# Cached log-forget sums, decay factors and past convolution moved to the front of a decoder layer, with its adaLN loads and key pages rearranged

## The chip, the cores and the metric

One Trainium2 chip, one of its cores. The metric is device time in microseconds of one execution of the program on that core; several executions of each kernel are timed and their median is given. The engines are TensorE (PE; its weight loads are listed as PEld), VectorE (DVE), ScalarE (ACT), GpSimd (POOL) and SyncE (SP). Each runs its own instructions in the order in which the program lists them, and waits where an operand is not ready. SP, POOL and ACT also issue DMAs.

## The reference

One layer of a decoder trunk, for 512 prompt tokens and 8 sample tokens that share the weights (520 columns in all, width 1024, 16 heads of 64):

```python
sh1, sc1, g1, sh2, sc2, g2 = ada_modulation(c, ada_w, ada_b)      # silu(c) @ ada_w + ada_b
h = rms_norm(x, norm1_g) * (1.0 + sc1) + sh1
xr, gr, q, k, v, fl, ga, gb = jnp.split(h @ w_in, cuts, axis=-1)
xc, conv_new = causal_dwconv(xr, conv_buf, conv_w, conv_b)
hr, h_last = rg_lru(xc, h0, pos0, ...)          # log_a = -8 * gate_r * softplus(-lam)
ya = (hr * gelu(gr)) @ w_proj_a
yb = attend(q, k, v, log_sigmoid(fl + b_f)) @ w_proj_b
x = x + g1 * ((sigmoid(ga) * ya + sigmoid(gb) * yb) @ w_o)
x = x + g2 * SwiGLU(rms_norm(x, norm2_g) * (1.0 + sc2) + sh2)
```

The attention adds to each logit the sum of log f from the key to the query. A sample token attends to 1024 cached positions, 8 pages of 128 out of a pool of 80, picked by a page table; its keys, values and log f are read through that table.

## The kernel before

Activations lie with features on the partitions, as 8 tiles of 128 x 520. Every fp32 product is made of three fp32r products: ACT rounds an operand to a high part (whi, hh), DVE subtracts to get the low part (wlo, hl), and PE multiplies hi x hi, lo x hi and hi x lo in two column halves of 260. The weights are cut into units of 128 output columns; a unit's product takes PE 48 matmuls.

The start. SP loads the parameters (prm), constants (cs), x and the page table (ptb, idx); ACT squares x (sq), DVE adds the squares, PE sums them over the partitions (ss), ACT and DVE make the reciprocal root (r) and DVE normalises x (xn). Meanwhile eight pieces of ada_w (araw) come in through the pool pgp of seven buffers and PE makes the first half of the modulation from them (adaf, transposed in adaft). From these come mod and n1amp, then h (hh, hl). q is computed in two halves of the inner dimension: the first (qp) starts when four tiles of h and the first w_in pieces (wraw, split by `q_weights`) are there.

After q the units follow in a list written out by hand: xr (with its convolution on DVE, `conv`), ga, gb, gr, for eight tiles, with the RG-LRU's gates, exponentials and scans between them; then k, v and the attention; then pb, wo and the FFN (fig, fiu, fo). In the background runs the past of the sample tokens. At each of the first 42 units a step `tick` works off key pages that have landed (DVE multiplies a page by q, L663 and L667, and sums over each head, L664 and L668), lets softmax and value steps run, and issues as many key pages as the table KEYS says, on POOL's queue up to unit 40 and on SP's after it. The pages share the pool pgp with the ada_w pieces. `VALUES` lists the units at which a value page is used.

The pieces that the change moves:

- `past_load` (L369) fetches the log f of the 64 pages (lfp, 0.5 MB) with one indirect DMA on POOL, into one of the two wraw buffers. `past_turn` (L380) transposes it on PE (lft), copies it (lk), and POOL adds up, page by page from the last, what lies after each page (after). `past_sums` (L395) multiplies lk by a triangle and after by ones on PE (suf): the sum of log f from each key to the end. The softmax over the past first needs suf. They are called in the loop of q's units (i = 4, 6, 7) and after the first two gb units.
- `decay` (L599) makes from lambda the factors of the RG-LRU's exponent, with a polynomial `log1p` of small DVE operations on 128 x 8; first needed by `lru_exp`. `past_conv` (L807) makes the part of the convolution that the stored state gives; first needed in `conv`. Both are called at i = 6 of q's loop.
- `ada_load(1, 6)` issues the seventh ada_w piece of the second third of the modulation, after both gb units of the first round; `ada_piece(1, 6)` uses it on PE at the beginning of the next round.

The order in which instructions stand on each engine comes from a scheduler; it follows the code, but lets work that it holds ready go ahead.

Of the kernel before, what the change touches and what calls it, by code (L numbers as in the profile page):

```python
# [8 lines left out]
F32 = mybir.dt.float32  # L9
F32R = mybir.dt.float32r  # L10
I32 = mybir.dt.int32
# [8 lines left out]
NS = 8  # L20
# [4 lines left out]
KT = 8  # L25
# [39 lines left out]
def kernel(ctx, tc, xT, par, gates, b_f, cst, cse, own, cache_k, cache_v, cache_lf, pt,  # L65
# [103 lines left out]
    def flush():  # L169
        while stores:  # L170
# [1 line left out]

    later = {}

    KEYS = dict(zip(range(42), (2, 2, 2, 0, 3, 3, 3, 2, 1, 1, 1, 1, 2, 2, 2, 1, 0, 1, 0, 1, 2, 2, 2, 2, 1, 1, 1, 1, 2, 2, 1, 2,
                                1, 2, 1, 2, 1, 2, 1, 2, 1, 0)))
    VALUES = (19, 21, 23, 25, 27, 29, 31, 35, 37, 39)
    LAST_POOL = 40

# [180 lines left out]
        dve.tensor_scalar(t[:, t0:e_], t[:, t0:e_], amp[:, f, 0:1], mod[:, shf, f, 0:1], ALU.mult, ALU.add)  # L360


    ptb = keep.tile([1, NS * NPAGE], I32, name="ptb")
    sp.dma_start(ptb, pt.rearrange("a b -> (a b)")[None, :])
    idx = keep.tile([NS * NPAGE, 1], I32, name="idx")
    sp.dma_start(idx, pt.rearrange("a (b c) -> (a b) c", c=1))
    lfp = []

    def past_load():  # L369
# [100 lines left out]
    def wraw():  # L470
        return wp.tile([128, KT, 256], F32, name="wraw", tag="wraw", bufs=2)

    ssq = [bank(f"ss1_{j}") for j in range(2)]
    for f in range(KT):
        t = slot("sq1")
# [6 lines left out]
            for j, (t0, t1) in enumerate(HALVES):  # L482
                pe.matmul(ssq[j][:, :HALF], lhsT=ones, rhs=sq[:, t0:t1], start=f == 3, stop=f == KT - 1)
    acc = [bank(f"adaf{fh}") for fh in range(2)]
    first_mod(0, acc[0], range(KT))
    r1 = slot("r1")
    for j, (t0, t1) in enumerate(HALVES):
        act.activation(r1[:, t0:t1], ssq[j][:, :HALF], AF.Sqrt, bias=eps, scale=1.0 / D)
        dve.reciprocal(r1[:, t0:t1], r1[:, t0:t1])
    for f in range(KT):  # L490
        t = slot("xn")
        dve.tensor_tensor(t, x[f], r1, ALU.mult)
        xn.append(t)
# [28 lines left out]
    raw = wraw()  # L522
    q_weights(1, raw, 0, 4)
    load_chunks(0)
    sp.dma_start(cs[:, C_TRI:], cst[:, C_TRI:])


    def log1p(name, e, n, out):
        z, z2, t = (small(name + s, 128, n, 1) for s in "abc")
        dve.tensor_scalar(t, e, 2.0, None, ALU.add)  # L530
        dve.reciprocal(t, t)
        dve.tensor_tensor(z, e, t, ALU.mult)
        dve.tensor_tensor(z2, z, z, ALU.mult)
        dve.tensor_scalar(t, z2, 2.0 / 17.0, 2.0 / 15.0, ALU.mult, ALU.add)
        for k in (13, 11, 9, 7, 5, 3, 1):
            dve.tensor_tensor(t, t, z2, ALU.mult)
            dve.tensor_scalar(t, t, 2.0 / k, None, ALU.add)
        dve.tensor_tensor(out, t, z, ALU.mult)

    qtd = drp.tile([NS, D], F32, name="qtd")  # L540
    fld = drp.tile([H, NT], F32, name="fld")
# [47 lines left out]
    def sum_forget():  # L589
# [6 lines left out]
    cl = keep.tile([128, KT], F32, name="cl")  # L596
    cneg = keep.tile([128, KT], F32, name="cneg")

    def decay():  # L599
        le = small("le", 128, KT, 1)  # L600
        ll = small("ll", 128, KT, 1)
        act.activation(le, prm[:, :, P_LAM], AF.Abs)
        act.activation(le, le, AF.Exp, scale=-1.0)
        log1p("lz", le, KT, ll)
        dve.tensor_scalar(le, prm[:, :, P_LAM], -1.0, 0.0, ALU.mult, ALU.max)
        dve.tensor_tensor(le, le, ll, ALU.add)
        dve.tensor_scalar(cl, le, -8.0, None, ALU.mult)
        dve.tensor_scalar(cneg, le, 8.0, None, ALU.mult)


    S = []
# [193 lines left out]
    conv_past = keep.tile([128, KT, NS], F32, name="conv_past")  # L805

    def past_conv():  # L807
        t = slot("cvp", KT * 24).rearrange("p (k s n) -> p k s n", k=KT, s=NS)
        for i in range(KT):
            dve.tensor_tensor(t[:, i], prm[:, i, P_SC:P_SC + 24].rearrange("p (s n) -> p s n", n=3),  # L810
                              prm[:, i, P_CW:P_CW + 3].unsqueeze(1).to_broadcast([128, NS, 3]), ALU.mult)
        dve.tensor_reduce(conv_past, t, AX.X, ALU.add)

    gws = {}

    gate_raw = {}
# [163 lines left out]
    for i in range(0, KT, 2):  # L980
        conv(i)
        if i == 0:
            q_done(*q_last)
        else:
            if i == 2:
                ada_piece(1, 6)
                ada_load(1, 7)
            both(lru_root, i - 2)
            gelu(i - 2)
            lru_scan(i - 2)  # L990
        conv(i + 1)
        if i:
            if i == 2:
                ada_piece(1, 7)
                ada_copy(1)
            gelu(i - 1)
            lru_scan(i - 1)
            both(lru_mul, i - 2)
            both(lru_g, i - 2)
        if i < 6:  # L1000
            gate_a(i)
            lru_gates(i)
            if i == 2:
                ada_end(1)
            gate_a(i + 1)
            lru_gates(i + 1)
            gate_b(i)
            if i == 0:
                past_sums(0)
            gate_b(i + 1)  # L1010
            if i == 0:
                past_sums(1)
                ada_load(1, 6)
            both(lru_exp, i)
            if i == 2:
                log_forget()
            if i == 4:
                sum_forget()
        else:
            lru_gates(i)  # L1020
            gate_a(i)
            lru_gates(i + 1)
            gate_a(i + 1)
            both(lru_exp, i)
            gelu(i)
            both(lru_root, i)
            gelu(i + 1)
            both(lru_scan, i)
            both(lru_mul, i)
            both(lru_g, i)  # L1030
# [556 lines left out]
```

## Time and profile before

| | |
|---|---|
| runs | 1068.85, 1069.54, 1070.95 us; median 1069.54 |
| the profiled execution's own time | 1067.71 us, span 1066.1 us |
| busy in the span | PE 1021.3, DVE 664.0, ACT 494.2, POOL 202.2 us |
| mean granted clock of PE | 0.987 |
| DMA | 206.95 MB, 194 GB/s over the span |

Times are microseconds from the start of the span. A row of a wait list names the waiting engine and line, then what it waited for, then the total, the number of waits and the longest. A row of a timeline has start, duration, engine, line, operation, output<-input and count; in brackets stands the idle time before it and what ended it. A row of a tile's list has the number of instructions, then the shortest, median and longest duration in ns and the first and last start in us.

### The profile page before, as it was taken

The numbers are of one execution on the slowest core, as the hardware profiler recorded it, in microseconds if no ns is written. First come the engines' busy times: TensorE is split into PE (matmuls) and PEld (weight loads), VectorE is DVE, ScalarE is ACT, GpSimd is POOL, SyncE is SP. The second block draws the span as 40 slices with busy tenths as digits, with TensorE's granted clock in tenths as the row PEclk, the third lists the DMA queues.
The fourth block names the chain that finished last, engine by engine and source line by source line (L and its number), as shares of the span: only waits on it lengthen the run. The fifth ranks groups of instructions, "written<-read, shape, count | busy, mean of one in ns | idle before, by whom it ended". The sixth has DMA issues, their size and how long they took to land.

```text
span 1066.1 us, 21006 instructions
## 1 busy us (share of the span) xinstructions
PE 1021.3 (96%) x8210; PEld 948.1 (89%) x8210; DVE 664.0 (62%) x1166; ACT 494.2 (46%) x976; POOL 202.2 (19%) x348
## 2 busy tenths in 40 slices
PE   4999899999999999999999999999999999999994
PEld 2888779999998987888898989999999999999993
DVE  5447999988999986656765447733343333443363
ACT  4423565757782367767783235523212232123251
POOL 0224511112134234544400014100000000000022
PEclk9999899999999999999999999999999999999998
DMA  9898887778788998987746852232333332332212
GB/s 327 281 320 286 279 297 208 260 240 297 255 283 280 351 314 263 259 252 250 248 172 216 313 166 70 73 88 79 109 90 80 97 102 80 95 104 80 72 55 74
DMA packets 165285, 206.95 MB, mean 194 GB/s; under 512 B 9778, under 2 KB 126018, under 8 KB 165122
## 3 DMA queue, kind: packets, MB, share of 16 engines
q1 hardware_dynamic: 147746, 149.90, 45.6%
q0 software_dynamic: 13760, 49.29, 13.6%
q10 hardware_dynamic: 3680, 6.42, 1.6%
q8 instruction: 64, 1.05, 0.4%
q14 instruction: 35, 0.29, 0.1%
HBM read 192.49 MB, written 13.09 MB: 193 GB/s over the span
## 4 chain that ended last, share of the span: by engine, by line
PE 76%; DVE 9%; issue 4%; DMA 4%; ACT 4%; POOL 2%; POOLq 1%; SPq 0%; ACTq 0%; DVEq 0%
PE fiu L245 11%; PE fig L245 11%; PE fo L245 9%; PE pb L245 4%; PE k L245 4%; PE v L245 4%; PE pa L245 3%; PE gr L245 3%; PE gb L245 3%; PE ga L245 3%; PE xr L245 3%; PE wo L245 3%; PE pv L751 3%; DMA wraw<-in_w_in_dram 2%; PE qp L467 2%
## 5 line engine op out<-in xcount | busy, mean ns | idle before, releaser
L211 DVE TENSOR_TENSOR wlo<-wraw,whi 128x1024 fp32r<-128x1024 f32 (+1 forms) x131 | 160.7, 1227 | 159.3 <-ACT whi L210 153.2
L210 ACT CAST whi<-wraw 128x1024 fp32r<-128x1024 f32 (+1 forms) x131 | 136.7, 1043 | 242.7 <-PE fo L245 74.6
L337 POOL TENSOR_TENSOR ss<-ss,sq 128x260 f32<-128x260 f32 x18 | 13.6, 756 | 419.5 <-ACT sq L336 419.0
L245 PE MATMUL fiu<-h2h,wlo 128*128 128x260 f32 x320 | 90.5, 283 | 0.0
L245 PE MATMUL fig<-h2h,wlo 128*128 128x260 f32 x320 | 90.5, 283 | 0.0
L245 PE MATMUL fig<-h2l,whi 128*128 128x260 f32 x320 | 90.2, 282 | 0.0
L245 PE MATMUL fiu<-h2l,whi 128*128 128x260 f32 x320 | 90.2, 282 | 0.0
L245 PE MATMUL fig<-h2h,whi 128*128 128x260 f32 x320 | 90.2, 282 | 0.0
L245 PE MATMUL fiu<-h2h,whi 128*128 128x260 f32 x320 | 90.2, 282 | 0.0
L245 PE MATMUL fo<-ach,whi 128*128 128x260 f32 x292 | 82.8, 284 | 0.0
L245 PE MATMUL fo<-ach,wlo 128*128 128x260 f32 x292 | 82.5, 282 | 0.0
L245 PE MATMUL fo<-acl,whi 128*128 128x260 f32 x292 | 82.3, 282 | 0.0
L622 POOL DMA_DIRECT2D pg<-in_cache_k_dram x79 | 42.1, 533 | 115.8 <-DVE S L668 61.1
L245 PEld LDWEIGHTS fiu<-h2h,whi 128*128 128x128 f32 x320 | 60.2, 188 | 0.0
L245 PEld LDWEIGHTS fig<-h2h,whi 128*128 128x128 f32 x320 | 60.2, 188 | 0.0
L245 PEld LDWEIGHTS fig<-h2l,whi 128*128 128x128 f32 x320 | 60.2, 188 | 0.0
L245 PEld LDWEIGHTS fiu<-h2l,whi 128*128 128x128 f32 x320 | 60.2, 188 | 0.0
L245 PEld LDWEIGHTS fig<-h2h,wlo 128*128 128x128 f32 x320 | 60.1, 188 | 0.0
L245 PEld LDWEIGHTS fiu<-h2h,wlo 128*128 128x128 f32 x320 | 60.1, 188 | 0.0
L667 DVE TENSOR_TENSOR pg<-pg,qb 128x1024 f32<-128x1024 f32 x48 | 57.4, 1213 | 1.1 <-DMA pg<-in_cache_k_dram 1.0
L668 DVE TENSOR_REDUCE S<-pg 128x16 f32<-128x1024 f32 x48 | 57.2, 1207 | 0.0
L245 PEld LDWEIGHTS fo<-ach,wlo 128*128 128x128 f32 x292 | 55.1, 189 | 0.0
(388 smaller groups left out, 3445.6 us busy)
## 6 DMA issues: line engine op xcount, KB each, us to landing
araw<-in_ada_w_dram SPq DMA_DIRECT2D x48, 512.0 KB, 6.3
pg<-in_cache_k_dram POOLq DMA_DIRECT2D x47, 512.0 KB, 5.6
wraw<-in_w_fi_dram SPq DMA_DIRECT2D x44, 512.0 KB, 4.0
pg<-in_cache_v_dram SPq DMA_DIRECT2D x42, 512.0 KB, 4.9
wraw<-in_w_in_dram SPq DMA_DIRECT2D x34, 512.0 KB, 8.4
wraw<-in_w_in_dram SPq DMA_DIRECT2D x11, 1024.0 KB, 7.9
pg<-in_cache_v_dram POOLq DMA_DIRECT2D x22, 512.0 KB, 5.5
pg<-in_cache_k_dram POOLq DMA_DIRECT2D x32, 256.0 KB, 5.4
```

The costliest lines, as they stand in the source:

```text
L210: state["act"] = act.copy(hi[:, :k1 - k0], src)
L211: state["last"] = dve.tensor_tensor(lo[:, :k1 - k0], src, hi[:, :k1 - k0].bitcast(F32), ALU.subtract)
L245: state["mm"] = pe.matmul(out[:, :HALF], lhsT=wt[k], rhs=at, start=k == 0 and m == 0, stop=k == nk - 1 and m == 2)
L337: eng.tensor_tensor(acc[:, t0:t1], acc[:, t0:t1], q_, ALU.add)
L467: state["mm"] = pe.matmul(b[:, :HALF], lhsT=wt, rhs=at[:, t0:t1], start=k == 0 and m == 0, stop=k == 3 and m == 2)
L622: done.append(eng.dma_start(pg, cache[bass.ds(r, 1), :, c0:c1].rearrange("a p c -> (a p) c")))
L667: dve.tensor_tensor(pg, pg, q, ALU.mult)
L668: dve.tensor_reduce(S[r // 2][:, c:c + H], pg.rearrange("p (h d) -> p h d", d=DH), AX.X, ALU.add)
L751: pe.matmul(pv[0][32 * gq:32 * gq + 32, :], lhsT=pw[r][:, c:c + 32], rhs=pgs[gq // 2][:, 512 * hf:512 * hf + 512], start=j == 0, stop=j == ...
```

## The change

- The page table is loaded ahead of x instead of behind it, and 128 columns more of the constants (the triangle) come with the first load.
- `decay`, `past_conv` and `past_load` are called ahead of the sums of squares. `past_turn` for both halves stands ahead of the first modulation's matmuls, `past_sums(0)` after six and `past_sums(1)` after eight of the eight ada_w pieces.
- `ada_load(1, 6)` stands between the two gb units instead of behind them.
- KEYS: a key page moves from unit 29 to unit 16, and one from unit 33 to unit 40.

```diff
     sp.dma_start(prm, par)
-    sp.dma_start(cs[:, :C_TRI], cst[:, :C_TRI])
+    sp.dma_start(cs[:, :C_S16], cst[:, :C_S16])
+    ptb = keep.tile([1, NS * NPAGE], I32, name="ptb")
+    sp.dma_start(ptb, pt.rearrange("a b -> (a b)")[None, :])
+    idx = keep.tile([NS * NPAGE, 1], I32, name="idx")
+    sp.dma_start(idx, pt.rearrange("a (b c) -> (a b) c", c=1))
...
-    KEYS = dict(zip(range(42), (2, 2, 2, 0, 3, 3, 3, 2, 1, 1, 1, 1, 2, 2, 2, 1, 0, 1, 0, 1, 2, 2, 2, 2, 1, 1, 1, 1, 2, 2, 1, 2,
-                                1, 2, 1, 2, 1, 2, 1, 2, 1, 0)))
+    KEYS = dict(zip(range(42), (2, 2, 2, 0, 3, 3, 3, 2, 1, 1, 1, 1, 2, 2, 2, 1, 1, 1, 0, 1, 2, 2, 2, 2, 1, 1, 1, 1, 2, 1, 1, 2,
+                                1, 1, 1, 2, 1, 2, 1, 2, 2, 0)))
...
+    decay()
+    past_conv()
+    past_load()
     ssq = [bank(f"ss1_{j}") for j in range(2)]
...
     acc = [bank(f"adaf{fh}") for fh in range(2)]
-    first_mod(0, acc[0], range(KT))
     r1 = slot("r1")
...
+    past_turn(0)
+    past_turn(1)
+    first_mod(0, acc[0], range(6))
+    past_sums(0)
+    first_mod(0, acc[0], range(6, KT))
+    past_sums(1)
     for f in range(KT):
         t = slot("xn")
...
         if i == 4:
-            past_load()
             split_upto(1)
             close = forget_logits()
         if i == 6:
             close()
-            with tc.issue_after(state["last"].ins), tc.issue_after(state["act"].ins):
-                decay()
-                past_conv()
-            past_turn(0)
-        if i == 7:
-            past_turn(1)
...
             gate_b(i)
             if i == 0:
-                past_sums(0)
+                ada_load(1, 6)
             gate_b(i + 1)
-            if i == 0:
-                past_sums(1)
-                ada_load(1, 6)
```

(The definitions of `log1p`, `decay` and `past_conv` move up in the file, unchanged.)

How it moves instructions. DVE at the start, from the reciprocal of the norm (r) to the first low part of h (hl), before:

```order
L489 RECIPROCAL r_192<-r_192 128x260 x2
L492 TENSOR_TENSOR xn<-x,r_192 128x520 x8
L429 TENSOR_TENSOR mod<-adaft_223,prm 128x2x2x9 x2
L433 SCALAR_TENSOR_TENSOR n1amp<-mod,prm 128x36
L458 TENSOR_TENSOR wlo<-wraw,whi 128x512 x2
```

and after the change:

```order
L528 RECIPROCAL r_192<-r_192 128x260 x2
L458 TENSOR_TENSOR wlo<-wraw,whi 128x512 x2
L458 TENSOR_TENSOR wlo<-wraw,whi 128x1024
L537 TENSOR_TENSOR xn<-x,r_192 128x520 x8
L458 TENSOR_TENSOR wlo<-wraw,whi 128x1024
L429 TENSOR_TENSOR mod<-adaft_321,prm 128x2x2x9 x2
L433 SCALAR_TENSOR_TENSOR n1amp<-mod,prm 128x36
```

The low parts of the first two weight pieces (three wlo) now stand ahead of the eight normalisations xn, and a third piece's ahead of mod.

PE at the start, from the sums of squares (ss) to q's first matmul (qp), before:

```order
L483 MATMUL ss_0_114<-sq_129,cs 128x260
L483 MATMUL ss_1_115<-sq_129,cs 128x260
L416 MATMUL adaf_142<-araw,silc 32x256 x32
L425 MATMUL adaft_223<-cs,adas 128x128 x2
L467 MATMUL qp_0_276<-hh,whi 128x260
```

and after the change:

```order
L523 MATMUL ss_1_163<-sq_177,cs 128x260
L383 MATMUL lft_197<-cs,lfp 128x64 x7
L383 MATMUL lft_217<-cs,lfp 128x64 x8
L416 MATMUL adaf_190<-araw,silc 32x256 x16
L398 MATMUL suf_273<-lk,cs 128x512
L416 MATMUL adaf_190<-araw,silc 32x256 x4
L398 MATMUL suf_290<-lk,cs 128x512
L416 MATMUL adaf_190<-araw,silc 32x256 x12
L399 MATMUL suf_273<-after,cs 128x512
L399 MATMUL suf_290<-after,cs 128x512
L425 MATMUL adaft_321<-cs,adas 128x128 x2
L467 MATMUL qp_0_374<-hh,whi 128x260
```

The transposes of the cached log f (lft) stand ahead of the first adaf, and the sums over what comes after each page (suf<-after) ahead of adaft and q.

SP's queue around the seventh and eighth ada_w pieces, which are loads (1, 6) and (1, 7), before:

```order
L186 DMA wraw<-in_w_in_dram 128x8x128 x4
L186 DMA wraw<-in_w_in_dram 128x8x256
L296 DMA araw<-in_ada_w_dram 128x1024 x4
L186 DMA wraw<-in_w_in_dram 128x8x256
L171 DMA mtd<-st 32x1
```

and after the change:

```order
L190 DMA wraw<-in_w_in_dram 128x8x128 x2
L622 DMA lf<-lfd 16x520
L300 DMA araw<-in_ada_w_dram 128x1024 x2
L190 DMA wraw<-in_w_in_dram 128x8x256
L300 DMA araw<-in_ada_w_dram 128x1024 x2
L190 DMA wraw<-in_w_in_dram 128x8x256
L175 DMA mtd<-st 32x1
```

The first two of the four araw loads went ahead of a load of weights.

More of the change, by code (lines that the diff above doesn't have):

```diff
@@ L360, in modulate @@
         dve.tensor_scalar(t[:, t0:e_], t[:, t0:e_], amp[:, f, 0:1], mod[:, shf, f, 0:1], ALU.mult, ALU.add)
[L363 to L366, printed above, removed]
     lfp = []
@@ L471, in wraw, with log1p, decay, past_conv @@
         return wp.tile([128, KT, 256], F32, name="wraw", tag="wraw", bufs=2)
+    def log1p(name, e, n, out):
+        z, z2, t = (small(name + s, 128, n, 1) for s in "abc")
+        dve.tensor_scalar(t, e, 2.0, None, ALU.add)
+        dve.reciprocal(t, t)
+        dve.tensor_tensor(z, e, t, ALU.mult)
+        dve.tensor_tensor(z2, z, z, ALU.mult)
+        dve.tensor_scalar(t, z2, 2.0 / 17.0, 2.0 / 15.0, ALU.mult, ALU.add)
+        for k in (13, 11, 9, 7, 5, 3, 1):
+            dve.tensor_tensor(t, t, z2, ALU.mult)
+            dve.tensor_scalar(t, t, 2.0 / k, None, ALU.add)
+        dve.tensor_tensor(out, t, z, ALU.mult)
+    cl = keep.tile([128, KT], F32, name="cl")
+    cneg = keep.tile([128, KT], F32, name="cneg")
+    def decay():
+        le = small("le", 128, KT, 1)
+        ll = small("ll", 128, KT, 1)
+        act.activation(le, prm[:, :, P_LAM], AF.Abs)
+        act.activation(le, le, AF.Exp, scale=-1.0)
+        log1p("lz", le, KT, ll)
+        dve.tensor_scalar(le, prm[:, :, P_LAM], -1.0, 0.0, ALU.mult, ALU.max)
+        dve.tensor_tensor(le, le, ll, ALU.add)
+        dve.tensor_scalar(cl, le, -8.0, None, ALU.mult)
+        dve.tensor_scalar(cneg, le, 8.0, None, ALU.mult)
+    conv_past = keep.tile([128, KT, NS], F32, name="conv_past")
+    def past_conv():
+        t = slot("cvp", KT * 24).rearrange("p (k s n) -> p k s n", k=KT, s=NS)
+        for i in range(KT):
+            dve.tensor_tensor(t[:, i], prm[:, i, P_SC:P_SC + 24].rearrange("p (s n) -> p s n", n=3),
+                              prm[:, i, P_CW:P_CW + 3].unsqueeze(1).to_broadcast([128, NS, 3]), ALU.mult)
+        dve.tensor_reduce(conv_past, t, AX.X, ALU.add)
+    decay()
+    past_conv()
+    past_load()
     ssq = [bank(f"ss1_{j}") for j in range(2)]
@@ L524 @@
     load_chunks(0)
[L525 to L538, printed above, removed]
+    sp.dma_start(cs[:, C_S16:], cst[:, C_S16:])
     qtd = drp.tile([NS, D], F32, name="qtd")
@@ L593, in sum_forget @@
         sp.dma_start(ftd, fcs)
[L596 to L608, printed above, removed]
     S = []
@@ L803, in q_samples @@
         store_now(qtd[:, 512 * b:512 * b + 512], t)
[L805 to L812, printed above, removed]
     gws = {}
```

## The prediction

> **What bounds the kernel now.** I read the page's first part, then who waited for whom on PE, then the busy time of each engine in stretches, and last the first 30 us as a timeline.
>
> ```profile
> span 1066.1 us, 21006 instructions
> PE 1021.3 (96%) x8210; PEld 948.1 (89%) x8210; DVE 664.0 (62%) x1166; ACT 494.2 (46%) x976; POOL 202.2 (19%) x348
> ```
>
> PE is the bound: it is idle for 1066.1 - 1021.3 = 44.8 us in all. A change can gain by taking work off PE where PE is busy, or by removing idle time of PE. Where that idle time lies:
>
> ```profile
> PE ss L483 <- DVE sq L478: 10.5, 2, 9.5
> PE gate L915 <- DVE xcl L279: 2.8, 1, 2.8
> PE ada L308 <- DMA araw<-in_ada_w_dram: 2.3, 2, 1.8
> PE lgm L718 <- DVE dg L713: 1.8, 1, 1.8
> PE gate L915 <- ACT xch L278: 1.3, 1, 1.3
> PE pa L245 <- DVE gl L279: 1.1, 2, 0.6
> PE ga L245 <- DVE wlo L211: 0.9, 1, 0.9
> ```
>
> The columns are the wait in total, how often, and the longest. The first row is the start. Rows 2, 3, 5 and 7 are waits between 100 and 155 us and make 2.8 + 2.3 + 1.3 + 0.9 = 7.3 us. The other two (2.9 us) come near 300 to 320 us. In the stretches (PE, PEld, DVE, ACT, POOL busy, granted clock, DMA share, GB/s) the reason for them is DVE:
>
> ```profile
> 100.00:150.00 50.00, 44.91 (x331) 42.34 (x330) 48.36 (x72) 24.37 (x46) 20.27 (x38) 0.93 0.88 284
> 150.00:200.00 50.00, 47.67 (x382) 44.24 (x381) 49.97 (x69) 30.22 (x56) 7.39 (x14) 1.00 0.81 253
> 200.00:250.00 50.00, 50.00 (x413) 46.99 (x412) 45.44 (x65) 31.96 (x59) 7.91 (x15) 1.00 0.75 237
> 250.00:300.00 50.00, 50.00 (x410) 46.73 (x409) 47.60 (x60) 40.28 (x67) 9.52 (x19) 1.00 0.85 270
> ```
>
> DVE has no spare time from 100 to 200 us and a little (4.6 and 2.4 us) from 200 to 300. Two engines are near their limit there, and PE is the one with the shorter slack.
>
> **The start, where the change loses.** The timeline of DVE, ACT, SP's queue and PE (start, duration):
>
> ```profile
> 14.39 3.41 DVE L489 RECIPROCAL r<-r 128x260 f32<-128x260 f32 x2 [1.84 <-ACT r L488]
> 17.84 4.97 DVE L492 TENSOR_TENSOR xn<-x,r 128x520 f32<-128x520 f32 x8
> 23.82 1.14 ACT L457 CAST whi<-wraw 128x512 fp32r<-128x512 f32 x2 [0.40 <-DMA wraw<-in_w_in_dram]
> 24.87 0.81 ACT L439 ACTIVATE hh<-xn,mod,n1amp 128x512 fp32r<-128x512 f32 x1
> 25.67 1.05 ACT L457 CAST whi<-wraw 128x1024 fp32r<-128x1024 f32 x1
> 27.45 1.22 DVE L458 TENSOR_TENSOR wlo<-wraw,whi 128x1024 fp32r<-128x1024 f32 x1
> 5.61 0.35 SPq L364 DMA_DIRECT2D ptb<-in_pt_dram  x1
> 6.48 0.57 SPq L366 DMA_DIRECT2D idx<-in_pt_dram  x1
> 20.96 0.64 PE L416 MATMUL adaf<-araw,silc 128*32 128x256 f32 x8 [0.72 <-DMA araw<-in_ada_w_dram]
> 22.35 0.64 PE L416 MATMUL adaf<-araw,silc 128*32 128x256 f32 x8 [0.74 <-DMA araw<-in_ada_w_dram]
> 25.73 0.58 PE L467 MATMUL qp<-hh,whi 128*128 128x260 f32 x1 [1.81 <-ACT hh L439]
> ```
>
> Now DVE normalises x (xn, 17.84 to 22.8) while the weights are still under way: the first piece of wraw lands at 23.82, and q starts at 25.73. The change's DVE order puts the three wlo of the first two pieces ahead of the eight xn. Engines run in order, so xn, which needs only x and r, waits for the second weight piece. That is the dearest effect of the change, and the diff doesn't show it; the order does.
>
> When the second piece lands: ptb and idx are issued ahead of x, 0.35 + 0.57 us and the steps between, so x starts about 1 us later; of this I charge 0.7 (bounds 0 and 1), since SP issues x faster than it is transferred. The 64 KB more of cs are 0.2 us. The cached log f is 0.52 MB more in front of the weights. How long that occupies the DMA engines is seen where it is fetched now (queues in the stretch 56 to 66 us):
>
> ```profile
> q1 hardware_dynamic: 2123, 2.81, 80.8%
> q0 software_dynamic: 80, 0.52, 21.4%
> lfp<-in_cache_lf_dram,idx POOLq DMA_INDIRECT x1, 8.2
> ```
>
> It is alone on q0: 21.4% of 10 us are 2.1 us; at the rate of q1 in the same rows (2.81 MB in 8.1 us) it would be 1.5 us. I take 1.5. Together 2.4 us: the first piece at 26.2 and the second 1.4 us later (spacing of the two adaf rows above, each opened by a 512 KB load), at 27.6. Then follow in series whi 1.05, wlo 1.22, xn 4.97, wlo 1.22, mod and n1amp 0.43, hh 0.81: 9.7 us, so q starts at 37.3 instead of 25.73, **11.6 us later**. Lowest: only the 1.5 us of log f in front, 10.7. Highest: the eighth ada_w piece is issued only when PE has used the first (seven buffers), and in PE's new order the 16 lft transposes stand ahead of that. ss, whose first matmul comes at 9.5 now (row 1 of the waits), is held by x and by some 30 small DVE operations of decay and convolution (0.15 us each at the shortest, rows below) ahead of the sums of squares; I estimate its end near 17.5, the transposes' near 19.6, the issue near 20.3, before the seventh piece has landed (now 20.96, then near 23.4). This costs nothing, unless it slips by 2 us: then a load of at least 3.7 us
>
> ```profile
> DMA to landing us min/median/max: 3.7/6.3/12.1
> ```
>
> from issue (araw's row) puts both pieces 1.2 us later: 12.8. POOL's additions (5.2 us and two copies, below, from about 20 us) and the suf sums behind them end near 28 to 29 us, ahead of the mod that waits for xn: they are hidden, but only because xn is late.
>
> **What it wins on PE.** The moved matmuls stood where PE was busy:
>
> ```profile
> 85.41 1.09 PE L383 MATMUL lft<-cs,lfp 64*128 64x64 f32 x8
> 86.43 1.07 PE L308 MATMUL ada<-araw,silc 128*32 128x512 f32 x8
> 135.38 0.28 PE L245 MATMUL gb<-hl,whi 128*128 128x260 f32 x1
> 135.50 1.02 PE L398 MATMUL suf<-lk,cs 128*128 128x512 f32 x2
> 137.34 0.28 PE L245 MATMUL gb<-hh,wlo 128*128 128x260 f32 x1
> ```
>
> Eight transposes hold PE from 85.41 to 86.43, twice: 2.0 us. One turn of suf sums holds it from 135.50 to 137.22 (the next matmul's start less one step of 0.12), twice: 3.4 us. **5.4 us** leave PE's busy stretch for a time in which it idles anyway.
>
> **What it wins in waits.** Off POOL, which issues the key pages in the same queue, go
>
> ```profile
> L392 POOL TENSOR_TENSOR after<-after,lk x12: 406/430/1373, 95.5 to 111.1; 128x64 f32<-128x64 f32 x12
> POOL after L390 <- ACT lk L385: 4.0, 1, 4.0
> DVE pg L663 <- DMA pg<-in_cache_k_dram: 5.5, 2, 4.4
> ```
>
> 12 x 0.43 = 5.2 us of additions, the copies before them and a wait of 4.0 us, with pages queued behind. DVE, which waits 5.5 us for pages, gets them earlier; its own operations of decay go too:
>
> ```profile
> L536 DVE TENSOR_TENSOR lzc<-lzc,lzb x7: 148/294/516, 94.5 to 108.3; 128x8 f32<-128x8 f32 x7
> L537 DVE TENSOR_SCALAR lzc<-lzc x7: 153/298/393, 95.0 to 109.8; 128x8 f32<-128x8 f32 x7
> 72.09 16.67 DMA wraw<-in_w_in_dram
> ```
>
> At 7 x (0.29 + 0.30) they are at most 4.1 us; by the shortest, 2.1. The last row is of the chain that ended last: a weight chunk issued at 72.09 and landing at 88.76, while lfp holds one of the two wraw buffers. Without lfp there the chunk behind it can start as soon as its own buffer is free. DVE is then some 5 us earlier at the first convolution (its operations and part of the 5.5 us), and the gate matmuls' 2.8 + 1.3 us and the 0.9 us for wlo go. The 2.3 us for araw: ada_load(1, 6) stands one unit (5.8 us) earlier, two loads in front of a wraw load on SP; if their buffers are late, wraw waits behind them. I expect 6.5 of the 7.3 us to go, and 1 of the later 2.9: **7.5 us**, between 3 and all 10.2.
>
> The two moved pages:
>
> ```profile
> L667 DVE TENSOR_TENSOR pg<-pg,qb 128x1024 f32<-128x1024 f32 x48 | 57.4, 1213 | 1.1 <-DMA pg<-in_cache_k_dram 1.0
> ```
>
> Product and sum take 1.2 us of DVE each, so 2.4 us go from unit 29 to 16 and as much from 33 to 40. This costs nothing, as long as the 4.6 + 2.4 us of idle DVE between 200 and 300 cover them; 2.4 us a page if not. The page at unit 40 goes from POOL's to SP's queue, where a wraw load stands behind it; 0 to 1 us.
>
> **The sum** against the profiled execution (1067.71 us, its span and 1.6 us around it): +11.6 - 5.4 - 7.5 = -1.3 us, 1066.4. That execution lies 1.8 us below the median of the three runs, so the median goes from 1069.5 to **1068.2**. About 0.2% (2.1 us) is what a measurement of this kernel can tell from no change. My forecast lies inside that.
>
> **Rivals.**
>
> - DVE stays late (slower). Its order still puts eight page products and four weight splits ahead of the first convolution, and the DMA is at 0.88 of its time there. If the chunk at 72.09 lands as late as now, the convolution ends only some 2 us earlier (decay's operations at their shortest), while PE arrives 3 us earlier (2.0 of transposes, 0.9 of wlo). The gate wait then stays, and the araw wait with it. The point: the first xcl against PE's arrival at the gate matmuls, both counted from q's start. Only about 1.5 of 10.2 us go: +11.6 - 5.4 - 1.5 = +4.7, 1074.2. Against it: lfp's buffer and POOL's additions are gone.
> - All waits go and the start is at its lowest: 10.7 - 5.4 - 10.2 = -4.9, 1064.6. For it: DVE's idle time between 200 and 300 us can take the rest.
> - The front is hidden as the change says: q starts only 2.4 us later. 2.4 - 5.4 - 7.5 = -10.5, 1059.0. Against it stands DVE's order; xn could start at 18 us only if the weight pieces had landed by then, and the first lands at 23.82 even now.
> [...]
>
> [...]
>
> **How the numbers follow.** Forecast 0.48, DVE late 0.24, all waits gone 0.13, eighth piece late 0.10, front hidden 0.05. The forecast's own spread (10.7 to 12.8 at the start, 5 to 9 us of waits: -3.7 to +2.4) puts 0.45 of it below -2.1, 0.05 above. Faster: 0.22 + 0.13 + 0.05 and a little of the late piece = 0.41. Slower: nearly all of DVE late and a rest = 0.25. Same: 0.34. The range goes from all waits gone, 1064.4, to DVE late at 1074.0; what it leaves out is the hidden front and the far halves of those two.
>
> **What would show it.** Right: DVE's first xn after 28 us and qp's first matmul at 36 to 39; no lft or suf between matmuls after it; no gate or ada wait over 1 us; PE's idle time 1 to 4 us less in all but the start, which has 6 more. Wrong: qp before 32 (the front is cheaper), or gate L915 waits for xcl again (DVE late), or a new wait of PE for wraw behind the araw loads on SP.

## The result, and the profile after

The changed kernel takes 1078.98 us (median of five runs, 1077.53 to 1086.09) against 1068.85 for the kernel before on the same chip: 1.0108 times as long, 95% interval 1.0076 to 1.0140, about 11 us slower. That is above the range of the forecast (1064.4 to 1074.0). The execution that was profiled is the longest of the five, 1086.09 us, so 7 us of what its trace shows beyond the kernel before are not in the median. The experiments below carry the argument; this trace shows where to look.

The head of the page after:

```profile
span 1084.4 us, 21018 instructions
PE 1029.0 (95%) x8210; PEld 954.6 (88%) x8210; DVE 664.5 (61%) x1166; ACT 499.5 (46%) x979; POOL 195.4 (18%) x347
```

PE is idle for 55.4 us where it was idle for 44.8, and busy for 7.7 us more with the same 8210 matmuls: some of them ran slower. The waits of PE after, as a list (total, number, longest):

```profile
PE ss L523 <- DVE sq L518: 13.9, 2, 13.3
PE qp L467 <- ACT hh L439: 5.8, 1, 5.8
PE gate L916 <- ACT xch L282: 3.3, 1, 3.3
PE ga L249 <- DVE pw L738: 3.1, 1, 3.1
PE adaft L425 <- ACT adas L422: 2.5, 1, 2.5
PE gate L916 <- ACT gate L917: 2.1, 1, 2.1
PE ada L312 <- DMA araw<-in_ada_w_dram: 2.0, 1, 2.0
```

Rows 1, 2 and 5 are the start. Row 3 is the convolution, still waited for; row 7 the araw load, still waited for. Rows 4 and 6 are new: one begins at 188 us, one at 301 us (where the kernel before stands near 289). Two stretches (PE, PEld, DVE, ACT, POOL busy, granted clock, DMA share, GB/s):

```profile
100.00:150.00 50.00, 46.43 (x364) 44.84 (x364) 41.24 (x62) 23.22 (x46) 15.94 (x29) 0.93 0.79 255
150.00:200.00 50.00, 44.85 (x323) 41.26 (x322) 50.00 (x67) 29.95 (x52) 6.89 (x13) 0.90 0.78 249
```

DVE stands idle for 8.8 us between 100 and 150 us (1.6 before) and has none to spare in the next 50 us, where PE gets through 323 matmuls (382 before) at a granted clock of 0.90. The start, on ACT, DVE and PE (start, duration, idle time before in brackets):

```profile
27.20 1.14 ACT L457 CAST whi<-wraw 128x512 fp32r<-128x512 f32 x2 [6.30 <-DMA wraw<-in_w_in_dram]
29.79 1.23 DVE L458 TENSOR_TENSOR wlo<-wraw,whi 128x1024 fp32r<-128x1024 f32 x1 [0.64 <-ACT whi L457]
30.93 4.97 DVE L537 TENSOR_TENSOR xn<-x,r 128x520 f32<-128x520 f32 x8
18.34 1.94 PE L383 MATMUL lft<-cs,lfp 64*128 64x64 f32 x15
38.27 0.59 PE L467 MATMUL qp<-hh,whi 128*128 128x260 f32 x1 [5.83 <-ACT hh L439]
```

xn does wait for the second weight piece, and q starts 12.5 us later than before. The table shows how far each unit then lies behind (+) or ahead of (-) the kernel before, in us, read from the first matmul of each (second column: its start in the kernel before). The later columns are experiments, described below; the executions read there lie within 2.5 us of their medians, that of the changed kernel 7.1 us above.

| unit | before | after | s1 | s16 | s17 | s13 | s6 | s7 |
|---|---|---|---|---|---|---|---|---|
| qp | 25.7 | +12.5 | +9.2 | +5.2 | +4.9 | +4.8 | +0.6 | -0.2 |
| q, second half | 52.2 | +12.0 | +9.8 | +3.2 | +2.9 | +2.9 | +0.9 | -0.4 |
| xr, first | 95.5 | +9.9 | +7.6 | +2.5 | +1.7 | +2.0 | +1.1 | -0.4 |
| gb, first | 129.7 | +8.3 | +0.6 | -5.6 | -5.9 | -6.0 | +1.2 | -0.4 |
| xr, second pair | 144.3 | +5.1 | -2.5 | -8.6 | -9.0 | -9.0 | +1.2 | -0.4 |
| gr, first | 155.0 | +4.4 | -4.7 | -10.9 | -4.0 | -10.4 | +2.1 | -3.8 |
| ga, second pair | 174.4 | +5.8 | -1.7 | -8.4 | -3.5 | -10.3 | +3.0 | -3.8 |
| gb, second pair | 189.3 | +11.8 | +3.4 | -2.8 | -2.4 | -9.1 | +3.0 | +0.9 |
| ga, last pair | 281.2 | +12.2 | +3.9 | -2.1 | -2.3 | -9.0 | +3.6 | +0.9 |
| gr behind it | 295.6 | +15.6 | +5.8 | -0.1 | -2.3 | -9.1 | +7.1 | +0.9 |
| k, third | 401.6 | +16.7 | +6.7 | +0.0 | -2.5 | -10.6 | +8.2 | +2.6 |
| fi | 666.8 | +17.7 | +7.5 | +1.2 | -2.8 | -9.3 | +8.0 | +2.5 |

Column "after": 12 us are lost at the start, 7.6 of them are back at 155 us, and then the gain is given away again: 6.0 us between 174 and 189, 3.4 at 281 to 295 (times of the kernel before). Smaller steps follow, back and forth; they were not looked into.

**At 188 us.** DVE and PE of the changed kernel, then its granted clock in stretches of one us (PE, PEld, DVE, ACT, POOL, clock):

```profile
190.74 0.41 DVE L736 TENSOR_TENSOR S<-S,lgm 128x256 f32<-128x256 f32 x1
187.51 0.60 PE L324 MATMUL adat<-cs,adas 128*128 128x128 f32 x4
191.21 0.58 PE L249 MATMUL ga<-hh,whi 128*128 128x260 f32 x1 [3.10 <-DVE pw L738]
```

```profile
189.00:190.00 1.00, 0.00 (x0) 0.00 (x0) 1.00 (x2) 0.98 (x2) 0.00 (x0) 1.00 0.02 8
192.00:193.00 1.00, 1.00 (x7) 1.00 (x6) 1.00 (x6) 0.98 (x3) 0.00 (x0) 0.50 0.86 315
196.00:197.00 1.00, 1.00 (x6) 1.00 (x6) 1.00 (x2) 0.19 (x1) 0.53 (x1) 0.50 0.71 160
```

The ga matmul starts 0.06 us after DVE has read the PSUM tile lgm of the softmax over the past (190.74 to 191.15), so I take it that it waits for that bank, though the row names the memset pw beside it. The code agrees: the pool has eight banks, and between lgm and this ga it takes seven (two for the first ga, four for gates, one for adat). DVE reads lgm that late because its queue is full: it is never idle from 178 us up to that read, and 4.9 us of that time are products and sums of key pages. The wait is 3.1 us, and PE runs at half speed (granted clock 0.50, where the trace lists a ga matmul with 0.42 us; at 1.00 with 0.28) for some 6 us behind it: 6.0 us in all. A clock of 0.50 stands behind 3.1 us of recorded wait here, and behind the 2.1 us of row 6 (from 303 to 306 us) and of s6 below. The same two instructions before the change:

```profile
181.04 0.40 DVE L719 TENSOR_TENSOR S<-S,lgm 128x256 f32<-128x256 f32 x1
182.06 0.37 PE L245 MATMUL ga<-hh,whi 128*128 128x260 f32 x1
```

DVE is done with lgm at 181.44 and PE comes at 182.06: 0.6 us apart. If it is this bank, every microsecond beyond 0.6 that PE gains ahead of this place without DVE is handed back here; s7 and s8 below bear that out.

### The profile page after: what moved, and what is told of

It reads as the page before. It is cut to its first block, busy times and chain, and to the rows that moved or that the text cites. A ratio compares the mean times of both kernels' runs of the same rounds, so it can differ in the third digit from the quotient of the medians.

```text
span 1084.4 us, 21018 instructions
## 1 busy us (share of the span) xinstructions
PE 1029.0 (95%) x8210; PEld 954.6 (88%) x8210; DVE 664.5 (61%) x1166; ACT 499.5 (46%) x979; POOL 195.4 (18%) x347
## 4 chain that ended last, share of the span: by engine, by line
PE 64%; DVE 9%; ACT 4%; issue 3%; POOL 1%; DMA 1%; POOLq 0%; ACTq 0%; DVEq 0%; SPq 0%
PE fiu L249 11%; PE fig L249 11%; PE fo L249 8%; PE pb L249 4%; PE v L249 4%; PE k L249 3%; PE gb L249 3%; PE pa L249 3%; PE wo L249 3%; PE pv L768 2%; PE ga L249 2%; PE po L1191 2%; DVE wlo L215 2%; PE ptt L1157 1%; DVE pg L684 1%
```

## The experiments

Each was timed in five rounds beside the kernel before (1068.4 to 1069.6 us in these sets); r is the ratio of its time to that kernel's with the 95% interval, and 0.1% is 1.07 us.

### The start, and ACT's wait for fa

While reading the trace I first took another wait for the cause of the later loss. ACT and SP of the changed kernel:

```profile
119.58 0.26 ACT L614 ACTIVATE fe<-fa 128x65 f32<-128x65 f32 x1 [13.83 <-DMA fa<-fld]
106.42 0.39 SPq L190 DMA_DIRECT2D wraw<-in_w_in_dram  x1
106.91 0.53 SPq L613 DMA_DIRECT2D fa<-fld  x1
```

The forget logits' reload fa now stands on SP behind a weight piece that waits for its buffer, and ACT, whose queue has fe ahead of the first xr's evacuation, waits 13.8 us for it (1.2 before). It looks dear. Four kernels test it: **s1** queues the low parts of the first weight pieces behind xn; **s2** queues fe where the code calls it, near 180 us; **s3** is both; **s4** puts fa and fe into the kernel before as they are in the changed one.

```diff
# s1
+    with tc.issue_after(xl.ins):          # xl: the last xn
         q_weights(0, raw, 0, 0)
# s2
+                with in_place():
                     log_forget()
# s4, on the kernel before (in short)
+        with tc.issue_after(state["lds"][2].ins):   # a load of wraw
             sp.dma_start(a, flat(fld))
...
+            with tc.issue_after(state["fe"].ins):
                 act.copy(xr[:, t0:t1], b)
...
+    log_forget()                          # ahead of the first conv, no longer at i == 2
     for i in range(0, KT, 2):
         conv(i)
```

> The changed kernel with one order mended: the low parts of the first weight pieces (wlo) are queued on DVE behind the eight xn. Theory A (two separate losses: the start, and a later one that has nothing to do with it): q's first matmul moves from 38.3 us to 32 to 34 us (it then waits for adaft, at 32.0 in the changed kernel, and mod, n1amp and hh behind it), so the run gains 4 to 6 us and comes to 1073 to 1075; ACT still waits more than 10 us for fa, and the gate and ga waits of PE past 120 us stay. Rival B (the later loss only follows from the late start, since the transfers and the units are out of step): the whole loss of 10 us goes, 1067 to 1070. Rival C (the start is hidden behind something later): under 2 us, 1077 to 1079.

> The changed kernel with only this mended: ACT's two operations on the forget logits (fe, which wait for the load fa) are queued where the code calls them, behind the weight split of that time (near 200 us), and not ahead of the first xr's evacuation; DVE's polynomial on them moves likewise. The DMAs stay as they are. Theory A (ACT's 13.8 us wait for fa is the later loss: the convolution and the second half of q's rows for the pages come 13 to 15 us late, DVE idles 8 us and lacks them later): the offset of the units behind the kernel before is about +4 at the first gr and stays at +2 to +5 to the end, so the run gains 8 to 11 us, 1068 to 1071; q's first matmul stays at 38.3. Rival B (the later loss comes from the two moved pages or from the earlier araw pair): under 2 us, 1077 to 1080, with the ga wait for DVE at 190 us and the wait for gl at 300 us still there.

> Both of the two mendings above. Theory A: the gains add, 4 to 6 and 8 to 11 us: 1062 to 1066, faster than the kernel before (1068.9) by 3 to 7 us, as the forecast's sum without the start's 5 us would have it (-5.4 of PE work and -7.5 of waits against +6 to +8 at the start). Rival (the second mending replaces the first, since the two losses are one): 1068 to 1071, no faster than the better of the two alone.

> The kernel before, with the later loss put into it and nothing else of the change: the load fa is queued on SP behind one weight piece, ACT's two operations on it stay ahead of the first xr's evacuation, and the polynomial on DVE follows them as in the changed kernel. Theory A: fa lands behind that piece, at 106 to 112 us in place of 96.6, ACT evacuates the first xr up to 6 us later than 106.3, and DVE falls behind as in the changed kernel, though by less: slower by 3 to 8 us, 1072 to 1077. Rival B (the order of fa does not matter): within 1.5 us of the kernel before, 1067.5 to 1070.5.

Measured: s1 1074.25 us, r 1.0049 (1.0033 to 1.0064); s2 1080.96, r 1.0109 (1.0088 to 1.0130); s3 1075.64, r 1.0059 (1.0037 to 1.0080); s4 1073.74, r 1.0041 (1.0027 to 1.0055). The order of wlo and xn is worth 5 to 6 us, as theory A had it. The theory's other half fell: taking the 13.8 us wait away gains nothing, alone or with s1. In the trace of s2 (4.5 us below its median) the first gr starts 4.3 us ahead of the kernel before and the second ga pair 1.4 us ahead; behind it, where PE waits 3.8 us for DVE as at 188 us above, it is 3.9 us late. The time of s4 lies in theory A's range, but s4 did not do what it was for: fa landed 5.9 us after its issue and no wait for it is recorded. With it DVE's polynomial came forward into DVE's full stretch, and the waits for xcl and araw grew from 2.8 to 4.6 and from 2.3 to 5.1 us. What of s4's loss is the load and what the polynomial was not separated.

So a new theory, C: from 130 to 190 us DVE sets the pace, whatever PE gains ahead of that, and the page table costs something by itself.

### The pages, the araw pair, and DVE's load

**s5** is s1 with the old KEYS and the old place of `ada_load(1, 6)`; **s6** and **s7** are the kernel before with the new KEYS alone and with the new place alone. **s8** is s1, and **s11** the kernel before, without the product with q for four pages:

```diff
-                    dve.tensor_tensor(pg, pg, q, ALU.mult)
+                    if not 16 <= sum(summed) < 20:
+                        dve.tensor_tensor(pg, pg, q, ALU.mult)
```

> The changed kernel with xn ahead of wlo as in s1_xn_first, and with the old table KEYS and the old place of ada_load(1, 6): only the moved front is left of the change. Theory C (DVE, not PE, sets the pace from 130 to 190 us, so the front's 5.4 us of PE work bring nothing; and the later losses of s1, 0.7 us at the third ga pair, 2 us at 285 to 295 and 2.5 us around 400, come from the moved pages' other order of the softmax steps): the ga wait for pw near 188 us stays at 3 us or more, the gate wait for ACT's gate near 290 us goes, 1069.5 to 1072 against 1074.3 for s1. Rival D (the later losses come from the front too): 1073 to 1075.5, with the gate wait of 2.1 us still there.

> The kernel before with the new table KEYS alone. Theory C (the moved pages cost, by the order of softmax steps and by 2.4 us more of DVE at units 16 and 17): slower by 2 to 5 us, 1071 to 1074, with new PE waits between 225 and 300 us. Rival D (the pages cost nothing, as the prediction had it): 1067.5 to 1070.

> The kernel before with ada_load(1, 6) between the two gb units alone. Theory C and the prediction: the araw wait of 2.3 us near 153 us shrinks or stays, nothing else moves: 1066.5 to 1069.5. Rival E (the pair of loads on SP pushes the weight pieces behind it, and PE or DVE waits for them): slower by over 2 us, 1071 or more.

> s1_xn_first with the multiplication by q left out for four key pages (the 17th to the 20th that DVE works off, near 150 to 175 us), 4 x 1.13 = 4.5 us of DVE work less; their sums are still made. Theory C (DVE is the bound from 130 to 190 us): PE's wait for DVE near 188 us falls from 3.6 us to under 1 us, no half-speed stretch follows it, gb at 189 us starts 3.5 to 6 us earlier than in s1, and the run is 3 to 6 us faster than s1's 1074.3: 1068.5 to 1071.5. Rival F (that wait is one of order or of a transfer, not of DVE's load): the wait stays and the run is within 1.5 us of s1.

> The kernel before with the multiplication by q left out for the same four key pages as in s8_light; their sums are still made. Theory C (in the kernel before PE and DVE arrive together at 181 to 189 us, so DVE's 4.5 us less gain little there): 1066 to 1068.7, a gain of 0 to 2.5 us where s8_light gained 7.4. Rival F (work on DVE there costs as much in the kernel before): a gain of 4 us or more, 1065 or less.

Measured: s5 1070.53, r 1.0020 (1.0007 to 1.0034); s6 1073.88, r 1.0037 (1.0021 to 1.0053); s7 1070.74, r 1.0019 (1.0005 to 1.0033); s8 1066.83, r 0.9981 (0.9968 to 0.9994); s11 1069.22, r 0.9999 (0.9985 to 1.0013). Theory C had the side of each right but for s7, where I had expected no loss. Two details missed. s8 came out 2 us faster than I had said, though a wait of 2.1 us is left at this place in its trace (3.3 us above its median). And in s5 that wait is 0.8 us and not 3, since PE is already held for 6.3 us by araw near 150 us.

s8 and s11 are the sharpest pair. The same 4.5 us of DVE work, left out, are worth 7 us behind the moved front and nothing before the change. In s11 DVE reads lgm 4.0 us earlier and PE still comes at 182.8, without a wait:

```profile
177.04 0.40 DVE L720 TENSOR_TENSOR S<-S,lgm 128x256 f32<-128x256 f32 x1
182.79 0.37 PE L245 MATMUL ga<-hh,whi 128*128 128x260 f32 x1
```

s7 shows the other side: PE's wait for araw goes (column s7, from -0.4 to -3.8 at 155 us), DVE does not move, and

```profile
181.07 0.40 DVE L719 TENSOR_TENSOR S<-S,lgm 128x256 f32<-128x256 f32 x1
181.53 0.58 PE L245 MATMUL ga<-hh,whi 128*128 128x260 f32 x1 [3.00 <-DVE pw L721]
```

PE now waits 3.0 us at the place where it came just in time, and starts 0.06 us after the read of lgm, as in the changed kernel (0.05 in s8). With the slow matmuls behind it (0.42 us each up to 184.5 us, 0.28 from 184.9) 4.7 us are lost for 3.4 gained.

s6 shows what the pages cost (its trace lies 2.5 us above its median). ACT in the kernel before, around the gates of the last pair:

```profile
284.09 0.63 ACT L278 CAST gh<-ge 128x520 fp32r<-128x520 f32 x1 [0.41 <-DVE ge L946]
285.36 0.63 ACT L278 CAST gh<-ge 128x520 fp32r<-128x520 f32 x1 [0.64 <-DVE ge L946]
287.30 1.59 ACT L916 ACTIVATE gate<-gate,prm 128x260 f32<-128x260 f32 x4
```

and in s6, with PE's wait and the granted clock behind it:

```profile
290.77 1.05 ACT L210 CAST whi<-wraw 128x1024 fp32r<-128x1024 f32 x1 [1.94 <-PE ga L245]
291.72 0.62 ACT L278 CAST gh<-ge 128x520 fp32r<-128x520 f32 x1
293.66 1.58 ACT L916 ACTIVATE gate<-gate,prm 128x260 f32<-128x260 f32 x4
```

```profile
294.19 0.51 PE L915 MATMUL gate<-xch,gws 128*128 128x260 f32 x2 [2.09 <-ACT gate L916]
```

```profile
294.00:295.00 1.00, 0.81 (x6) 0.82 (x7) 1.00 (x2) 1.00 (x4) 0.24 (x1) 1.00 0.90 279
297.00:298.00 1.00, 1.00 (x6) 1.00 (x6) 1.00 (x2) 0.26 (x1) 0.00 (x0) 0.50 0.77 307
299.00:300.00 1.00, 1.00 (x10) 1.00 (x10) 1.00 (x2) 0.00 (x0) 0.05 (x1) 1.00 1.04 348
```

With two pages at other units the order on ACT is another: a weight split that waits for PE (whi) now stands between the two gh and ahead of the gate's sigmoid, which empties the banks that PE needs. On DVE a page's product stands ahead of the second ge there, 288.5 to 289.7 us; by which step the pages bring this order about was not followed. PE waits 2.1 us and runs at half speed (granted clock 0.50) from 295.6 to 299: 3.5 us. The wait is the same in the changed kernel (row 6 of the waits) and in s16, and is gone in s5.

### What of the front is worth having

**s9** is the kernel before with only `decay` and `past_conv` in front. **s10** is s1 with the old KEYS, but two pages taken from units 8 and 10 to 18 and 19, behind DVE's full stretch, with the new place of `ada_load(1, 6)`; **s12** is s10 with the old place; **s14** has s10's pages and load in the kernel before, with no front; **s15** is s10 with fe as in s2.

```diff
# in short: KEYS of s10, s12, s14, s15, against the kernel before
-units 8, 10: 1, 1      units 18, 19: 0, 1
+units 8, 10: 0, 0      units 18, 19: 1, 2
```

> The kernel before with only decay and past_conv called ahead of the sums of squares; log f, its sums, the page table, the ada_w piece and the pages stay where they were. Theory C (DVE is the bound from 100 to 190 us): 2 to 4 us of small DVE operations leave that stretch, at the start they cost q 0 to 2 us (they run while x loads), the gate waits for xcl and xch (2.8 and 1.3 us) shrink: 1065 to 1068.5. Rival G (the operations only fill gaps of DVE where they were, and push q where they are): 1069 to 1072.

> The changed kernel with xn ahead of wlo, the old table KEYS, and two of its pages taken out of units 8 and 10 and issued at units 18 and 19, behind the stretch in which DVE has no idle time; the new place of ada_load(1, 6) stays. Theory C: 4 x 1.2 us of DVE less ahead of 188 us, the ga wait for pw there falls from 3.6 us to under 1.5 us, and the order that cost 2 us near 290 us is gone with the new table: 1064 to 1068. Rival D (a page is paid for wherever it is worked off, or the softmax steps that follow from it come at a bad place): 1070 to 1074.

> s10_pages_later with ada_load(1, 6) back behind the second gb unit. Theory C: PE waits for araw near 152 us, up to 6 us as in s5_front_xn_only, since DVE no longer hides that: 1066 to 1070, 1 to 3 us above s10_pages_later. Rival H (the earlier load costs as much elsewhere as it gains, as it did in s7_before_ada_early): within 1 us of s10_pages_later.

> The kernel before (no front) with the two pages taken from units 8 and 10 to 18 and 19 and with ada_load(1, 6) between the two gb units. Theory C (DVE's load and the araw wait are what counts, and the front pays for its 5.4 us of PE work with 9 us of start): the araw wait near 153 us goes without a wait for pw in its place, 1064 to 1067, as good as s10_pages_later or better. Rival J (the front's work off PE is what makes s10 fast): 1068 to 1070.5.

> s10_pages_later with ACT's two operations on fa queued where the code calls them, as in s2_fe_in_place; ACT waits 8.8 us for fa in s10. Theory C (that wait only delays the first convolution, which is paid for by DVE's slack now that there is some): 0 to 2 us gained, 1063.4 to 1065.4. Rival K (the wait still holds back DVE's pages): 3 us or more gained, under 1062.4. Rival L (two table loads and the polynomial near 200 us cost more than the wait): over 1066.5.

Measured: s9 1069.08, r 0.9999 (0.9985 to 1.0014); s10 1065.36, r 0.9953 (0.9935 to 0.9972); s12 1068.57, r 0.9999 (0.9987 to 1.0012); s14 1065.87, r 0.9967 (0.9950 to 0.9983); s15 1065.87, r 0.9968 (0.9950 to 0.9986). s9 gains nothing and costs nothing. Theory C missed it; rival G's range holds its time, but not for G's reason, since q starts no later (the trace has 6.4 us of gate waits where 4.1 stood). s10 and s14 are as theory C had them, and nearly alike: with q 9.6 us late the front is worth little or nothing. What gains in s14 is the pages moved later, not earlier, together with the earlier load: the load alone cost 2 us (s7), and the pages alone were not run. s12 shows that the earlier araw load is worth 3 to 5 us as soon as DVE does not take them back (without it the trace has an araw wait of 6.4 us). s15 came out within 0.5 us of s10, in none of the three ranges: mending the wait for fa again gains nothing.

That left the start. In s10, q waits for the first modulation, whose copy adas stands on ACT behind the two suf copies, and these behind POOL's additions. **s13** is s10 with suf queued behind adas and adaft; **s16** is the changed kernel with the start's two mendings and nothing else; **s17** is s16 with the old KEYS and the old place of the load.

```diff
-    first_mod(0, acc[0], range(6))
-    past_sums(0)
-    first_mod(0, acc[0], range(6, KT))
-    past_sums(1)
+    first_mod(0, acc[0], range(KT))
...
+    with tc.issue_after(state["adas"].ins), tc.issue_after(state["adaft"].ins):
+        past_sums(0)
+        past_sums(1)
     q_weights(0, raw, 4, 2)
```

> s10_pages_later with the four suf matmuls on PE and their two copies on ACT queued behind the first modulation's copy and transposes (adas, adaft), which in s10 wait for POOL's additions until 31.4 us. Theory C (the start is paid in full, since the pages cannot start before q): q's first matmul at 31.5 to 33 us in place of 35.3, the run 2 to 4 us faster than s10's 1065.4: 1061.5 to 1063.5. Rival I (the late start is absorbed by the waits behind it): within 1 us of s10, 1064.4 to 1066.4.

> The changed kernel with both mendings of its start (xn ahead of wlo as in s1_xn_first, the suf matmuls and copies behind adas and adaft as in s13_suf_late); the new table KEYS and the new place of ada_load(1, 6) stay. Theory C (the start is paid in full, the pages' table costs some 4 to 5 us): q's first matmul at 30.5, 1074.3 - 6 = 1067 to 1069.5, about as fast as the kernel before, with the gate wait of 2.1 us near 290 us and a wait for pw near 188 us. Rival M (DVE ahead of 188 us takes the gain back): 1071 to 1074.

> The kernel before with the moved front alone, its start mended as in s16: old table KEYS, old place of ada_load(1, 6). Theory C (the start's gain is carried to the end): 1070.5 of s5 less 5 to 6 us, 1064 to 1066.5, that is 3 to 5 us faster than the kernel before; with s14_no_front's 3.3 us that makes up most of s13_suf_late's 9.8. Rival N (without the pages moved later PE waits for araw and pw as in s5, and the gain is taken back): 1068 to 1071.

Measured: s13 1059.32, r 0.9905 (0.9875 to 0.9934); s16 1067.71, r 0.9993 (0.9977 to 1.0009); s17 1066.13, r 0.9979 (0.9967 to 0.9991). The start in s10 and in s13:

```profile
32.86 0.38 ACT L421 COPY adas<-adaf 128x256 f32<-128x256 f32 x1
35.34 0.58 PE L466 MATMUL qp<-hh,whi 128*128 128x260 f32 x1 [1.36 <-ACT hh L438]
35.72 0.42 PE L466 MATMUL qp<-hh,wlo 128*128 128x260 f32 x1
```

```profile
26.32 0.37 ACT L421 COPY adas<-adaf 128x256 f32<-128x256 f32 x1 [5.57 <-PE adaf L415]
30.09 1.02 PE L398 MATMUL suf<-after,cs 128*128 128x512 f32 x2
30.55 0.68 PE L466 MATMUL qp<-hh,whi 128*128 128x260 f32 x1
31.07 0.28 PE L466 MATMUL qp<-hh,wlo 128*128 128x260 f32 x1
```

q starts 4.8 us earlier, and at 0.28 us a matmul, not 0.42, with the suf matmuls right ahead of it where s10 has 1.36 us of idle PE: 5 to 6 us for an order of four matmuls and two copies. s16 mends nothing but the start and is level with the kernel before; its trace shows where the front's gain goes:

```profile
PE ga L249 <- DVE pw L739: 3.8, 1, 3.8
```

s13 is 10 us faster than the kernel before, 6 faster than s14, which has the same pages and load but no front, and some 20 us faster than the changed kernel, more than I had expected of it: the front is worth having with its start in order and DVE relieved. s17's time lies in theory C's range, but its gain, 2.2 us, is smaller than the 3 to 5 us behind that range: with the araw load at its old place PE waits 6.6 us for it, as it did in s12.

## Why the prediction failed

- **The start, 11.6 us: right.** 12.5 at qp, by the step it named: three wlo ahead of xn (the second weight piece landed 1 us later than I had it). That POOL's additions and suf are hidden only because xn is late was right too: with xn mended alone q moves by 3.3 us (s1), with suf behind adas by 7.3 (s16). The two mendings show that the start is paid in full: 1.0108 to 1.0049 (s1), to 0.9993 (s16). These 11 to 12 us are more than q's 7.3. The second half of q starts 8.8 us earlier, since q no longer begins at half speed (0.42 us a matmul at a granted clock of 0.50 in the changed kernel, 38 to 43 us; 0.28 us a matmul in s16); where the rest comes from was not separated. A slip of 2 us of the eighth ada_w piece, for which the 12.8 and the chance of 0.10 stand, no run shows: in the changed kernel PE does not wait for that piece, and 15 of the transposes, behind ss and 13 us of idle PE, took 1.94 us at a granted clock of 1.00, about as long each as before (1.02 us for eight).
- **log f behind x: wrong, and cheap.** I let it line up behind x. In the changed kernel ACT waits for the seventh tile of x, and in s9, which has the same DVE work in front but no log f, it does not:

```profile
13.81 0.64 ACT L516 ACTIVATE sq<-x 128x520 f32<-128x520 f32 x1 [2.54 <-DMA x<-in_xT_dram]
16.31 2.10 PE L523 MATMUL ss<-sq,cs 128*128 128x260 f32 x4 [0.59 <-DVE sq L518]
```

```profile
6.71 4.66 ACT L515 ACTIVATE sq<-x 128x520 f32<-128x520 f32 x8
14.27 2.10 PE L522 MATMUL ss<-sq,cs 128*128 128x260 f32 x4 [0.19 <-DVE sq L517]
```

  The last ss is 2.0 us later. The load of log f is under way in that time (issued at 5.5 us, 9.1 us to landing); but x is also issued 1.0 us later than in s9, behind the page table, and the two were not separated. It was hidden here, since xn waited for the weights anyway.
- **5.4 us of PE work: right for suf, uncertain for the transposes.** Column "after" falls by 3.2 us from the first gb to the next xr, and the columns s1, s16, s17 and s13 by 3.0 or 3.1. From q to xr, where the transposes stood, "after" falls by 2.1, s1 by 2.2, but s16, s17 and s13 only by 0.7 to 1.2.
- **7.5 us of waits: wrong, and not only in size.** In the changed kernel the gate and araw waits stayed (3.6 and 2.0 us), where the prediction had wanted none over 1 us. With the start mended (s16) no gate wait is left ahead of 160 us, and PE gains 14.1 us from q to the first gr, more than the 5.4 and 7.3 of the forecast. But 8.1 of them are lost by 189 us. The step that failed is the first one: "A change can gain by taking work off PE where PE is busy, or by removing idle time of PE." On it rests the sum, which carries what PE gains ahead of 155 us to the end. The rows quoted under it said that DVE had almost no idle time from 100 to 200 us (1.6 us in 100); I counted PE's waits and never looked for the next place at which PE needs DVE. There the slack was 0.6 us: of the 8.1 us that PE of the changed kernel had gained by 155 us, 6.0 went there, and 3.4 at the wait that the moved pages brought. The time came out some 11 us longer, as by the start alone; of the 12.9 us of gain in the sum nothing was left.
- **The moved pages, "This costs nothing": wrong.** They cost 4 us in the kernel before (s6). I looked for idle DVE time between 200 and 300 us to cover 2.4 us a page; what they changed is ACT's order at 285 us. Behind the moved front, pages and load together cost less than the 4 and 2 us that they cost alone: 3 to 4 us (s1 against s5) and 1.5 (s16 against s17).
- **The araw load a unit earlier: wrong in sign.** A gain of up to 2.3 us was in the sum; alone it costs 2 us (s7), since what PE wins is lost again where it needs DVE.
- **Missing from the sum:** that a new wait costs more than its length. 3.1 us cost 6.0 (the changed kernel), 2.1 us cost 3.5 (s6).
- The rival "DVE stays late" was the nearest, with the right engine. Its price kept only the old waits; the new ones, the half speed behind them and the pages come on top. (The ends of the stated range lie 0.2 us below the rivals' own sums, 1064.6 and 1074.2; nothing hangs on it.)

Open: why the executions of the changed kernel spread over 8 us, what of s4's 4 us is the load and what the polynomial, and how two pages come to change ACT's order.

## What to carry to other kernels

Before a gain on the bound engine is summed, find the next place where that engine needs the second busy one, and measure the slack there: in this kernel the gain ended at that slack unless the second engine gained as well. An edit in a scheduled kernel is priced by its order on every engine: here two wrong neighbours in the front cost 11 to 12 us, and two pages that moved cost 4 through the order on ACT, which does no work on them. And price a wait with the slow stretch behind it (here 3.1 us cost 6.0).

## What the runs showed of the hardware

In s6 a wait of PE of 2.1 us was followed by 3.4 us at half speed (granted clock 0.50) that began only 1.4 us after PE had resumed. In the changed kernel, where eight pv matmuls (1.06 us) stand ahead of a wait of the same length, as in s6, the clock was 0.94 in the microsecond in which PE resumed (302 to 303 us) and 0.50 in the three behind it; what makes the difference was not separated. And DVE and POOL were slower side by side in the mended start. The tile xn and POOL's additions in the changed kernel, where they run apart, and in s13, where they run together:

```profile
L537 DVE TENSOR_TENSOR xn<-x,r x8: 694/695/696, 30.9 to 35.2; 128x520 f32<-128x520 f32 x8
21.22 4.26 POOL L392 TENSOR_TENSOR after<-after,lk 128x64 f32<-128x64 f32 x11
```

```profile
L533 DVE TENSOR_TENSOR xn<-x,r x8: 701/910/918, 21.4 to 27.0; 128x520 f32<-128x520 f32 x8
21.07 8.34 POOL L391 TENSOR_TENSOR after<-after,lk 128x64 f32<-128x64 f32 x11
```

xn takes 910 ns in place of 695, the eleven additions 8.34 us in place of 4.26. What slows them was not separated.
